# Places of expert 0 by counting ranks in the router loop, the remaining searches and the first down matrix moved behind the first gather

## The chip, the cores and the metric

The kernel runs on one core of one Trainium2 chip, as one launch. The metric is the device time in microseconds (us), smaller is better. The work is done by TensorE (PE in the profile: matrix products and transposes into PSUM, with the weight loads PEld beside them), VectorE (DVE), ScalarE (ACT), GpSimd (POOL) and the queues that start transfers (SP's, and POOL's own). Every engine runs its instructions strictly in the order that the program fixes when it is built.

## The reference, cut to what matters

One transformer block over 1024 tokens of width 1024: a mixer (gated linear attention beside a long convolution), a residual, and then a mixture of experts in which each expert picks its tokens. The change touches only the choice of tokens and what stands around it:

```python
aff  = softmax(h @ w_router)                      # 1024 tokens x 16 experts
vals, idx = top_k(aff.T, 128)                     # every expert takes its 128 best tokens
xs   = h[idx]                                     # gather, per expert 128 x 1024
hid  = silu(xs @ w_gate) * (xs @ w_up)            # per expert, 1024 x 1024 matrices
y    = (hid @ w_down) * vals
out  = zeros_like(h).at[idx].add(y)               # scatter-add, then residual and norm
```

The order of an expert's 128 tokens among themselves is free, as long as the same order is used for the gather, the values and the scatter.

## The kernel before, in words

Everything is float32. A product of two matrices is made of three products of rounded halves: `split` makes `hi` on ACT (L144) and `lo` on DVE (L147), `mm3` issues the three products on PE (L150 to L152). A weight matrix of an expert is loaded in 8 tiles of 128 x 1024 (`eraw` for gate and up, `erawl` for down), split into `ehi` and `elo`, and multiplied into a PSUM tile `pex`: 8 tiles, two halves, three products, so 48 `pex` products for a matrix and 144 for an expert's three. On PE the matrices come in the order gate(0), up(0), gate(1), down(0), up(1), gate(2), down(1) and so on. An expert's input needs a transposed copy of its gathered rows (`ptx` from `xs`, then `tt`, `thi`, `tlo`), and its down product a transposed copy of the hidden values (`ptx` from `sg`).

The router loop runs over the token tiles 7 down to 0: `gla_out`, `residual` and `router` are staggered, and `router(i)` ends with `aff[:, :, i]`, the 16 affinities of 128 tokens. When all of `aff` is there, `select(e0, ne, tag, bits)` finds for `ne` experts at once the 128th largest affinity bit by bit: each iteration compares `aff` with `2^bits - 1` thresholds (`gea` or `geb` on DVE), counts over the tokens with 8 products with a matrix of ones (`psel` on PE), and takes the largest threshold that still holds 128 tokens (`thr`, `base` on DVE). `select(0, 2, "a", 5)` takes 6 iterations, `select(2, 14, "b", 2)` takes 15. Then the mask (`gt`, `eq`, `need`, `keep`) and two rounds of prefix sums on PE give `pos`, the place of each token in its expert's list. `route(e)` turns `pos` into indices (`oh` on DVE, 8 small products `pi` on PE, `pv`, `ix`) and starts an indirect gather on POOL's queue. `tv` holds token numbers and the affinities in three bf16 parts for `pi`.

Two allocations matter here. The PSUM tag "t" has two buffers, which `pi` and `ptx` take in program order (and `psel` of search a before the change). The tag "ex" has three buffers of a full matrix, which `pex` takes, and `psel` of search b. `elo` has four buffers (`NLO`). The order within each engine is set by a list scheduler at build time, which follows data, buffers and estimated times; nothing is reordered when the kernel runs.

Of the kernel before, what the change touches and what calls it, by code (L numbers as in the profile page):

```python
# [10 lines left out]
F32 = mybir.dt.float32  # L11
# [9 lines left out]
P = 128  # L21
# [21 lines left out]
def shape_constants():  # L43
    f = np.float32
    out = {}
    quarter = D // 4
    omega = (1.0 / (f(10000.0) ** (np.arange(quarter, dtype=f) / f(quarter)))).astype(f)
    er = (np.arange(16, dtype=f)[:, None] * omega).astype(f)
    ec = (np.arange(64, dtype=f)[:, None] * omega).astype(f)
    out["posr"] = np.concatenate([np.sin(er), np.cos(er)], -1).astype(f)  # L50
    pc = np.concatenate([np.sin(ec), np.cos(ec)], -1).astype(f)
    out["posc"] = np.concatenate([pc, pc], 0)
    out["pos"] = np.concatenate([np.repeat(out["posr"], 64, 0), np.tile(out["posc"], (8, 1))], 1).reshape(8, 128, 1024)
    out["ident"] = np.eye(P, dtype=f)

    n1 = np.arange(8)[None, :, None]
    n2 = np.arange(128)[:, None, None]
    k2 = np.arange(128)[None, None, :]
    th = 2 * np.pi * (k2 + 0.5) * (n1 + 8 * n2) / 2048.0
    fc, fs = np.cos(th), -np.sin(th)  # L60
    out["fmat"] = np.stack([fc, fs], 1).astype(f)
    out["fneg"] = (-fs).astype(f)
    out["imat"] = np.stack([fc.transpose(2, 1, 0) / 1024.0, fs.transpose(2, 1, 0) / 1024.0], 1).astype(f)

    t = np.linspace(0.0, 1.0, L, dtype=f)[:, None]
    w = (f(2.0 * math.pi) * np.arange(L, dtype=f)[:, None] / f(L)).astype(f)
    bands = np.linspace(1e-4, 15, 16, dtype=f)[None, :]
    fw = (bands * w).astype(f)
    z = np.concatenate([t, np.cos(fw), -np.sin(fw)], -1).astype(f)
    n = (np.arange(8)[:, None] + 8 * np.arange(128)[None, :]).reshape(-1)  # L70
    out["zfeat"] = z[n].T.astype(f)
    deltas = np.abs(np.linspace(math.log(1e-2) / 1.5, math.log(1e-2) / 0.3, HYW, dtype=f))
    dec = np.exp(-t * deltas).astype(f)[n].reshape(8, 128, 4, 128)
    out["decay"] = dec.transpose(2, 1, 0, 3).astype(f)

    i16 = 1.0 / 16.0
    tok, col = np.meshgrid(np.arange(P), np.arange(2 * (CH + 2)), indexing="ij")
    pre = (tok // CH == col // (CH + 2)) & (tok % CH < col % (CH + 2))
    out["pre"] = (pre * i16).astype(f)
    ss, cc = np.meshgrid(np.arange(P) % CH, np.arange(CH), indexing="ij")  # L80
    out["smask"] = np.stack([ss <= cc, ss >= cc], 1).astype(np.int32)
    ss, cc = np.meshgrid(np.arange(P), np.arange(P), indexing="ij")
    out["before"] = (ss < cc).astype(f)
    out["slot"] = np.broadcast_to(np.arange(1, P + 1, dtype=f), (P, P)).copy()
    out["sel"] = np.tile(np.eye(32, E, dtype=f), (4, 1))
    tid = np.zeros((P, NT, 2), f)
    tid[:, :, 0] = np.arange(P)[:, None]
    tid[:, :, 1] = P * np.arange(NT)[None, :]
    out["tokid"] = tid
    for b in (5, 2):  # L90
        dig = np.zeros((P, 30 // b, 1 << b), np.int32)
        for i in range(30 // b):
            dig[:, i, :] = np.arange(1 << b) << (30 - b * (i + 1))
        out[f"digit{b}"] = dig
    return {"c_" + k: np.ascontiguousarray(v) for k, v in out.items()}
# [3 lines left out]
def tile_gla_hyena_moe(ctx: ExitStack, tc: tile.TileContext, io: dict, out: bass.AP):  # L99
# [826 lines left out]
    def wout_tile(k, tile_of, queue=SY):  # L926
        raw = mid_tile("woraw")
        queue.dma_start(raw, io["w_out"][0, k * P:(k + 1) * P, :])
        V.tensor_mul(raw, raw, m2)
        hi, lo = tile_of("wohi", F32R), tile_of("wolo", F32R)  # L930
        split(hi, lo, raw)
        return hi, lo
# [12 lines left out]
    def gb(tag, bufs):  # L945
        return lambda shape, name: psg.tile(shape, F32, name=name, tag=tag, bufs=bufs)

    ga, gc, gd, ge1 = gb("ga", 2), gb("gc", 2), gb("gd", 1), gb("ge", 1)

    def chunk_updates(i, e4, vs):  # L950
# [123 lines left out]
    befr = s2([P, P], name="befr")  # L1074
    SY.dma_start(befr, io["c_before"])
    V.tensor_copy(before, befr)
    ws = [wout_tile(k, op_tile) for k in range(4)]
    p2a.close()
    g2 = p2.enter_context(tc.tile_pool(name="g2", bufs=1, side="right", reuse_waits="tile"))

    def h4(shape, name, tag, bufs, dt=F32):
        return g2.tile(shape, dt, name=name, tag=tag, bufs=bufs)


    diag = [g2.tile([P, NH, P], F32, name=f"diag{x}") for x in range(2)]
# [98 lines left out]
        V.reciprocal(sm, sm)  # L1184
        V.tensor_scalar(aff[:, :, i], ex, sm, None, op0=ALU.mult)

    outs, rows = [], []
    for i in reversed(range(-2 - 1, NT)):
        if i >= 0:
            outs.append((i, gla_out(i)))  # L1190
        if rows:
            router(*rows.pop(0))
        if outs and (i < 0 or len(outs) > 1):
            o_ = outs.pop(0)
            rows.append((o_[0], *residual(*o_)))
    p2.close()
    st_stack.close()
    early_stack.close()
# [25 lines left out]
        queue.dma_start(raw, io[w][0, e, k * P:(k + 1) * P, :])  # L1224
        return raw

    loaded = {(w, k): expert_tile(w, 0, k) for w in ("w_gate", "w_up", "w_down") for k in range(KT)}

    def expert_mm(w, e, xt, between=None, at=KB):
        ps = pse.tile([P, D], F32, name="pex", tag="ex", bufs=3)  # L1230
# [14 lines left out]
    def select(e0, ne, tag, bits):  # L1245

        aff_ = aff[:, e0:e0 + ne]

        def tl(shape, dt, name, bufs=1):
            return mt(shape, dt, name + tag, name + tag, bufs)  # L1250

        def column_sums(ps, mask):
            for t in range(NT):
                T.matmul(ps, ones, mask[:, :, t], start=t == 0, stop=t == NT - 1)

        def prefix(ps, mask):
            T.matmul(ps, before, mask, start=True, stop=False)
            for s in range(1, NT):
                T.matmul(ps[:, :, s:], ones, mask[:, :, 0:NT - s], start=False, stop=s == NT - 1)

        if e0 == 0:
            def pr(n):
                return pT([P, n], "psel")
        else:
            acc = pse.tile([P, D], F32, name="psel", tag="ex", bufs=3)
            flip = [0]

            def pr(n):
                flip[0] ^= 512
                return acc[:, flip[0]:flip[0] + n]  # L1270

        base = tl([P, ne], F32, "base")
        V.memset(base, 0.0)
        nd = 1 << bits
        for b in range(30 // bits):
            thr = tl([P, nd, ne], F32, "thr", 2)
            V.tensor_tensor(thr.bitcast(I32), digit[bits][:, b, :, None].to_broadcast([P, nd, ne]),
                            base.bitcast(I32)[:, None, :].to_broadcast([P, nd, ne]), op=ALU.bitwise_or)
            ge = tl([P, nd - 1, ne, NT], BF16, "ge")
            V.tensor_tensor(ge, aff_[:, None].to_broadcast([P, nd - 1, ne, NT]),  # L1280
                            thr[:, 1:nd, :, None].to_broadcast([P, nd - 1, ne, NT]), op=ALU.is_ge)
            pc = pr((nd - 1) * ne)
            column_sums(pc, ge.rearrange("p q e t -> p (q e) t"))
            upper = thr[:, 1:nd].rearrange("p q e -> p (q e)")
            V.scalar_tensor_tensor(upper, pc, float(CAP) - 0.5, upper, op0=ALU.is_ge, op1=ALU.mult)
            V.tensor_reduce(base, thr.rearrange("p q e -> p e q"), AX.X, ALU.max)
        thb = base[:, :, None].to_broadcast([P, ne, NT])
        gt = tl([P, ne, NT], BF16, "gt")
        V.tensor_tensor(gt, aff_, thb, op=ALU.is_gt)
        eq = tl([P, ne, NT], BF16, "eq")  # L1290
        V.tensor_tensor(eq, aff_, thb, op=ALU.is_equal)
        pg_ = pr(ne)
        column_sums(pg_, gt)
        need = tl([P, ne], F32, "need")
        V.tensor_scalar(need, pg_, -1.0, float(CAP), op0=ALU.mult, op1=ALU.add)
        pq_ = pr(ne * NT).rearrange("p (e t) -> p e t", t=NT)
        prefix(pq_, eq)
        keep = tl([P, ne, NT], BF16, "keep")
        V.tensor_tensor(keep, pq_, need[:, :, None].to_broadcast([P, ne, NT]), op=ALU.is_lt)
        V.tensor_mul(keep, keep, eq)  # L1300
        V.tensor_add(keep, keep, gt)
        pp = pr(ne * NT).rearrange("p (e t) -> p e t", t=NT)
        prefix(pp, keep)
        V.scalar_tensor_tensor(pos[:, e0:e0 + ne], pp, 1.0, keep, op0=ALU.add, op1=ALU.mult)

    NF = 2
    select(0, NF, "a", 5)

    tv = mp.tile([P, E, NT, 5], BF16, name="tv")
    V.tensor_copy(tv[:, :, :, 0:2], tokid[:, None].to_broadcast([P, E, NT, 2]))  # L1310
# [8 lines left out]
    def route(e):  # L1319
        pi = pT([P, 5], "pi")  # L1320
        oh = mt([P, NT, P], BF16, "oh", "s2", NS)
        V.tensor_tensor(oh, slot[:, None, :].to_broadcast([P, NT, P]),
                        pos[:, e, :, None].to_broadcast([P, NT, P]), op=ALU.is_equal)
        for t in range(NT):
            T.matmul(pi, oh[:, t], tv[:, e, t], start=t == 0, stop=t == NT - 1)
        ix = tiny.tile([P, 1], I32, name="ix", bufs=4)
# [31 lines left out]

    A.preload_act_table_set("silu_and_others")
    routed = [route(0)]  # L1360
    xt = transposed(0, routed[0][2], True)
    routed.append(route(1))
    select(NF, E - NF, "b", 2)
    with tc.issue_after(routed[0][3].ins):
        sg = gate_part(0, xt)
    m5 = row_of(5, mp)
# [81 lines left out]
```

## Time and profile before

| what | value |
|---|---|
| time, median of 3 runs | 1380.2 us (1378.26 to 1383.59) |
| time of the profiled execution | 1380.59 us |
| its span, first to last instruction | 1378.8 us |
| mean granted TensorE clock | 0.964 |
| PE busy | 1276.7 us (93%) |
| DVE busy | 1149.8 us (83%) |
| ACT busy | 805.8 us (58%) |
| router loop and its tail | until 736 us |
| searches, first gather | 736 to 768 us |
| expert products | 768 to about 1353 us |

The profiled execution is one of the ordinary ones: its time is 0.4 us above the median, and 1.8 us of it lie outside the span. Times inside the span are given in us from its start. A row of the timeline gives start, duration, engine, line, operation, output and inputs, and in brackets how long the engine was idle before it and what released it. [...]

### The profile page before, as it was taken

How to read it: one execution, taken by the hardware profiler on the slowest of the kernel's cores; microseconds unless marked ns; L12 is line 12 of the kernel's file. 1: busy time of each engine (PE TensorE's matmuls, PEld its weight loads, DVE VectorE, ACT ScalarE, POOL GpSimd, SP SyncE). 2: the span in 40 equal slices, each digit the busy share in tenths (PEclk: the TensorE clock that was granted, in tenths of full speed). 3: DMA queues.
4: the chain of work that ended last, by engine and by line, in shares of the span. 5: the costliest groups of instructions: out<-in, count | busy, mean ns of one | idle time of the engine just before them, and what ended most of it. 6: DMA issues, size and time to landing. Idle time of an engine off the chain costs nothing.

```text
span 1378.8 us, 21543 instructions
## 1 busy us (share of the span) xinstructions
PE 1276.7 (93%) x7720; PEld 1044.5 (76%) x7720; DVE 1149.8 (83%) x1920; ACT 805.8 (58%) x1228; POOL 129.9 (9%) x142
## 2 busy tenths in 40 slices
PE   6988999999999998988996899999999999999982
PEld 4777888688898897766775678888888888877762
DVE  6877938899778678788656799999999999988886
ACT  3247453121211314886553678888888888877864
POOL 1020000010100110001000000001111111012010
PEclk9998999999999998999996899999999999999996
DMA  7993551774746545676768789999999999999765
GB/s 213 325 230 123 167 145 42 234 199 150 202 152 185 141 113 176 159 165 186 242 230 337 244 318 357 361 394 383 387 385 386 390 385 391 369 365 370 264 202 225
DMA packets 154362, 354.81 MB, mean 257 GB/s; under 512 B 28389, under 2 KB 74013, under 8 KB 153999
## 3 DMA queue, kind: packets, MB, share of 16 engines
q1 hardware_dynamic: 134911, 292.84, 59.7%
q0 software_dynamic: 19344, 60.61, 15.8%
q8 instruction: 60, 0.98, 0.3%
q14 instruction: 47, 0.39, 0.1%
HBM read 310.89 MB, written 50.89 MB: 262 GB/s over the span
## 4 chain that ended last, share of the span: by engine, by line
PE 70%; issue 9%; DMA 7%; DVE 7%; ACT 5%; POOL 1%; SPq 1%; POOLq 0%; DVEq 0%; ACTq 0%
PE pex L151 13%; PE pex L152 12%; PE pex L150 12%; PE phy L543 3%; PE phy L542 3%; PE phy L545 3%; PE ptx L1343 2%; PE pdft L467 2%; PE pdft L468 2%; PE pvg L150 2%; PE pm L334 2%; PE pvg L152 1%; PE pvg L151 1%; PE pdft L671 1%; DMA wt<-w_ada 1%
## 5 line engine op out<-in xcount | busy, mean ns | idle before, releaser
L147 DVE TENSOR_TENSOR elo<-eraw,ehi 128x1024 fp32r<-128x1024 f32 x256 | 302.5, 1221 | 13.2 <-issue 6.0
L151 PE MATMUL pex<-elo,thi 128*128 128x512 f32 x768 | 306.4, 399 | 4.8 <-DVE elo L147 4.4
L150 PE MATMUL pex<-ehi,thi 128*128 128x512 f32 x768 | 305.8, 398 | 2.3 <-ACT thi L144 1.3
L152 PE MATMUL pex<-ehi,tlo 128*128 128x512 f32 x768 | 303.4, 395 | 0.8 <-DVE tlo L147 0.8
L144 ACT ACTIVATE ehi<-eraw 128x1024 fp32r<-128x1024 f32 x256 | 265.0, 1068 | 50.2 <-PE pex L152 49.3
L151 PEld LDWEIGHTS pex<-elo,thi 128*128 128x128 f32 x768 | 145.3, 189 | 40.3 <-DVE elo L147 10.5
L150 PEld LDWEIGHTS pex<-ehi,thi 128*128 128x128 f32 x768 | 145.3, 189 | 33.9 <-ACT thi L144 1.7
L152 PEld LDWEIGHTS pex<-ehi,tlo 128*128 128x128 f32 x768 | 145.3, 189 | 31.6 <-DVE tlo L147 1.2
L147 DVE TENSOR_TENSOR elo<-erawl,ehi 128x1024 fp32r<-128x1024 f32 x128 | 149.5, 1221 | 6.2 <-ACT ehi L144 5.3
L144 ACT ACTIVATE ehi<-erawl 128x1024 fp32r<-128x1024 f32 x128 | 131.3, 1057 | 19.6 <-PE pex L152 17.4
L144 ACT ACTIVATE whi<-wraw 128x1024 fp32r<-128x1024 f32 x30 | 31.8, 1059 | 104.6 <-DMA wraw<-w_in 29.6
L542 PE MATMUL phy<-xh,whi 128*128 128x512 f32 x192 | 77.2, 402 | 12.2 <-ACT whi L144 12.2
L543 PE MATMUL phy<-xl,whi 128*128 128x512 f32 x192 | 76.1, 396 | 0.0
L150 PE MATMUL pvg<-whi,xh 128*128 128x256 f32 x256 | 73.3, 286 | 0.0
L151 PE MATMUL pvg<-wlo,xh 128*128 128x256 f32 x256 | 72.5, 283 | 0.0
L152 PE MATMUL pvg<-whi,xl 128*128 128x256 f32 x256 | 72.5, 283 | 0.0
L1389 POOL DMA_INDIRECT d_acc<-y,ix x15 | 34.6, 2308 | 392.4 <-DVE y L1388 392.4
L1348 ACT ACTIVATE tt<-ptx,fcol,gfcol 128x128 f32<-128x128 f32 x128 | 48.7, 463 | 34.1 <-PE ptx L1343 34.1
L545 PE MATMUL phy<-xh,wlo 128*128 128x512 f32 x192 | 61.9, 400 | 0.0
L438 ACT ACTIVATE D<-pdft 128x512 f32<-128x512 f32 x32 | 19.1, 597 | 70.9 <-PE pdft L468 40.7
L147 DVE TENSOR_TENSOR wlo<-wraw,whi 128x1024 fp32r<-128x1024 f32 x30 | 36.7, 1222 | 22.5 <-ACT whi L144 22.5
L467 PE MATMUL pdft<-kk,fmat 128*128 128x128 f32 x256 | 52.7, 289 | 0.3 <-ACT D L438 0.2
(452 smaller groups left out, 2601.1 us busy)
## 6 DMA issues: line engine op xcount, KB each, us to landing
eraw<-w_gate SPq DMA_DIRECT2D x128, 512.0 KB
eraw<-w_up SPq DMA_DIRECT2D x128, 512.0 KB
erawl<-w_down SPq DMA_DIRECT2D x128, 512.0 KB
wt<-w_ada SPq DMA_DIRECT2D x48, 512.0 KB
wraw<-w_in SPq DMA_DIRECT2D x30, 512.0 KB
kspec<-d_spec SPq DMA_DIRECT2D x16, 512.0 KB
xt<-x SPq DMA_DIRECT2D x8, 512.0 KB
d_spec<-ue POOLq DMA_DIRECT2D x8, 512.0 KB, 6.0
```

What stands on the lines that cost most here:

```text
L144: A.activation(hi, src, AF.Copy)
L147: V.tensor_sub(lo, src, hi.bitcast(F32))
L150: T.matmul(out_, lh, rh, start=first, stop=False)
L151: T.matmul(out_, lh, rl, start=False, stop=False)
L152: T.matmul(out_, ll, rh, start=False, stop=last)
L334: T.matmul(pm[32 * g:32 * g + 32, 256 * h:256 * h + 256], sc[:, k], wt[:, 256 * g:256 * g + 256], start=k == ks[0] and h == 0, stop=k == k ...
L467: T.matmul(ps[:, r], fmat[:, r, m1], kk[m1 // 4][:, 0, m1 % 4], start=True, stop=False)
L542: T.matmul(ps[:, h], hi[:, k], rh[k][:, h], start=k == 0, stop=False)
L543: T.matmul(ps[:, h], hi[:, k], rl[k][:, h], start=False, stop=False)
L545: T.matmul(ps[:, h], lo[:, k], rh[k][:, h], start=False, stop=k == KT - 1)
L1348: A.activation(tt[:, k], pt[:, k], AF.Identity, bias=fcol[:, 0, kk_:kk_ + 1], scale=gfcol[:, kk_:kk_ + 1])
L1389: G.indirect_dma_start(out=d_acc[:, :], out_offset=bass.IndirectOffsetOnAxis(ap=ix[:, :1], axis=0), in_=y, in_offset=None, compute_op=ALU.add)
```

## The change

Four things are edited.

- `rank(i)` and `rank_sums(i, over)` are new, for the first `NF = 1` expert. In the router loop, a tile behind `router`, the affinities of expert 0 in tile i are laid along a row (`prow`, a transpose on PE; `arow`), and every token of tile i is compared with all tokens of tiles i to 7 (`over` on DVE, 128 to 1024 columns, with the count in `cnt`; `tie` breaks equal values inside the tile by the constant `after`). `rank_sums`, a tile later, subtracts from the ranks of the later tiles what the products `pbelow` of `over` with a column of ones say. Over the loop these are 8 transposes and 28 small products. At the end `pos0` is the place of every token for expert 0, without a search.
- `route(0)` takes `pos0`. The `select` for the first two experts is gone from the place before `tv`. Expert 1 alone is searched by `select(1, 1, "a", 5)`, which stands behind `transposed(0)` in the program; `route(1)` and `select(2, 14, "b", 2)` follow as before.
- All searches now keep `psel` in a tile of the tag "ex".
- The 8 tiles of w_down of expert 0 are loaded by POOL's queue behind the first gather, and no longer by SP's queue ahead of it.

```diff
+    arow = g2.tile([P, NF, L], F32, name="arow")
...
+    def rank(i):
+        W = (NT - i) * P
+        for e in range(NF):
+            row = gc([P, P], name="prow")
+            T.transpose(row, aff[:, e, i:i + 1].to_broadcast([P, P]), ident)
+            V.tensor_copy(arow[:, e, i * P:(i + 1) * P], row)
+            a_ = aff[:, e, i:i + 1]
+            over = h4([P, L], "over", "over", 2, BF16)
+            cnt = tiny.tile([P, 2], F32, name="cnt")
+            V.tensor_scalar(over[:, 0:W], arow[:, e, i * P:], a_, 0.0, op0=ALU.is_gt, op1=ALU.add, accum_out=cnt[:, 0:1])
+            tie = s2([P, P], BF16, name="tie")
+            V.scalar_tensor_tensor(tie, arow[:, e, i * P:(i + 1) * P], a_, after, op0=ALU.is_equal, op1=ALU.mult,
+                                   accum_out=cnt[:, 1:2])
+            V.scalar_tensor_tensor(rk[:, e, i:i + 1], cnt[:, 0:1], cnt[:, 1:2], rk[:, e, i:i + 1], op0=ALU.add, op1=ALU.add)
+            overs.append((i, over))
+
+    def rank_sums(i, over):
+        if i + 1 < NT:
+            below = gc([P, NT], name="pbelow")
+            for t in range(i + 1, NT):
+                T.matmul(below[:, t:t + 1], over[:, (t - i) * P:(t - i + 1) * P], ones[:, 0:1], start=True, stop=True)
+            V.tensor_sub(rk[:, 0, i + 1:], rk[:, 0, i + 1:], below[:, i + 1:])
+        if i == 0:
+            V.scalar_tensor_tensor(pos0[:, 0], rk[:, 0], CAP + 0.5, rk[:, 0], op0=ALU.is_le, op1=ALU.mult)
...
         if rows:
+            ranks.append(rows[0][0])
             router(*rows.pop(0))
         if outs and (i < 0 or len(outs) > 1):
             o_ = outs.pop(0)
             rows.append((o_[0], *residual(*o_)))
+        while len(ranks) > 1 or ranks == [0]:
+            rank(ranks.pop(0))
+            if len(overs) > 1:
+                rank_sums(*overs.pop(0))
+    rank_sums(*overs.pop(0))
...
-    loaded = {(w, k): expert_tile(w, 0, k) for w in ("w_gate", "w_up", "w_down") for k in range(KT)}
+    loaded = {(w, k): expert_tile(w, 0, k) for w in ("w_gate", "w_up") for k in range(KT)}
...
-        if e0 == 0:
-            def pr(n):
-                return pT([P, n], "psel")
-        else:
-            acc = pse.tile([P, D], F32, name="psel", tag="ex", bufs=3)
...
+        acc = pse.tile([P, D], F32, name="psel", tag="ex", bufs=3)
...
-    NF = 2
-    select(0, NF, "a", 5)
...
-                        pos[:, e, :, None].to_broadcast([P, NT, P]), op=ALU.is_equal)
+                        (pos0[:, e] if e < NF else pos[:, e])[:, :, None].to_broadcast([P, NT, P]), op=ALU.is_equal)
...
     routed = [route(0)]
+    with tc.issue_after(routed[0][4].ins):
+        loaded.update({("w_down", k): expert_tile("w_down", 0, k, G) for k in range(KT)})
     xt = transposed(0, routed[0][2], True)
+    select(1, 1, "a", 5)
     routed.append(route(1))
-    select(NF, E - NF, "b", 2)
+    select(2, E - 2, "b", 2)
```

The scheduler moves more than the diff shows. On VectorE, at the end of search b, around the splits of expert 1's gate matrix and expert 0's down matrix, this stood before (`gtb`, `eqb`, `needb`, `keepb`, `pos`: the mask and places of experts 2 to 15):

```order
L1289 TENSOR_TENSOR gtb<-aff,baseb 128x112
L1291 TENSOR_TENSOR eqb<-aff,baseb 128x112
L1377 TENSOR_TENSOR sg<-pex,sg 128x1024
L1295 TENSOR_SCALAR needb<-psel 128x14
L147 TENSOR_TENSOR elo<-eraw,ehi 128x1024
L1299 TENSOR_TENSOR keepb<-psel,needb 128x112
L147 TENSOR_TENSOR elo<-eraw,ehi 128x1024
L1300 TENSOR_TENSOR keepb<-keepb,eqb 128x112
L147 TENSOR_TENSOR elo<-eraw,ehi 128x1024
L1301 TENSOR_TENSOR keepb<-keepb,gtb 128x112
L147 TENSOR_TENSOR elo<-eraw,ehi 128x1024
L1304 SCALAR_TENSOR_TENSOR pos<-psel,keepb 128x112
```

The same steps stand there now, from the last splits of the down matrix (`erawl`) on; the pattern of four rows from `geb` to `thrb` stands five times in all ahead of `gtb`, of which the first and last are shown:

```order
L148 TENSOR_TENSOR elo<-erawl,ehi 128x1024
L1316 TENSOR_TENSOR thrb<-digit_6047,baseb 128x56
L148 TENSOR_TENSOR elo<-erawl,ehi 128x1024
L1319 TENSOR_TENSOR geb<-aff,thrb 128x336
L1324 SCALAR_TENSOR_TENSOR thrb<-psel,thrb 128x42
L1325 TENSOR_REDUCE baseb<-thrb 128x14
...
L1319 TENSOR_TENSOR geb<-aff,thrb 128x336
L1324 SCALAR_TENSOR_TENSOR thrb<-psel,thrb 128x42
L1325 TENSOR_REDUCE baseb<-thrb 128x14
L1328 TENSOR_TENSOR gtb<-aff,baseb 128x112
L1330 TENSOR_TENSOR eqb<-aff,baseb 128x112
L1334 TENSOR_SCALAR needb<-psel 128x14
```

Before, the steps of the search lie between splits; now the last five iterations and the mask stand in a row behind the fourth split of the down matrix, with nothing else between them.

On TensorE, where the transposes of the hidden values of expert 0 (`ptx` from `sg`) stand, before, with the last of the products that place expert 2 (`pi`) ahead of them; the `pex` around them are the last of gate(1):

```order
L1325 LDWEIGHTS oh
L1325 MATMUL pi<-tv,oh 128x5
L151 MATMUL pex<-elo,thi 128x512
L152 MATMUL pex<-ehi,tlo 128x512
L1343 MATMUL ptx<-ident,sg 128x128 x4
L150 MATMUL pex<-ehi,thi 128x512
L1343 MATMUL ptx<-ident,sg 128x128 x4
L151 MATMUL pex<-elo,thi 128x512
L152 MATMUL pex<-ehi,tlo 128x512
```

and now, where the `pex` behind them are the first of down(0):

```order
L1302 LDWEIGHTS ones
L1302 MATMUL psel<-keepb,ones 128x14
L1362 LDWEIGHTS oh
L1362 MATMUL pi<-tv,oh 128x5
...
L1380 MATMUL ptx<-ident,sg 128x128 x8
L151 MATMUL pex<-ehi,thi 128x512
L152 MATMUL pex<-elo,thi 128x512
L153 MATMUL pex<-ehi,tlo 128x512
```

Before, 132 `pex` stand ahead of the first of these transposes and 12 more before down(0) begins. Now all 144 stand ahead, and between the 144th and the transposes stand, with no `pex` among them, five groups of `psel` for `geb`, those for `gtb`, `eqb` and `keepb`, and the 8 `pi` of expert 2. Ahead of the first `pex` there are now 3 groups for `gea` and 2 for `geb` (before 6 and 9); between the first and the 144th there are 3 groups for `gea` (at the 7th, 19th and 32nd `pex`), 8 for `geb`, and the small ones for `gta`, `eqa`, `keepa` (before 6 for `geb` and the small ones for `gtb`, `eqb`, `keepb`). `pi` of expert 1 stands at the 60th `pex` (before the 2nd), `ptx` of expert 1 at the 81st (before the 66th).

On POOL's queue the first gathers stood in a row before:

```order
L1159 DMA d_h<-hh 128x1024
L1151 DMA d_acc<-xres 128x1024
L1159 DMA d_h<-hh 128x1024
L1333 DMA xs<-d_h,ix 128x1024 x3
L1389 DMA d_acc<-y,ix 1024x1024
```

and now:

```order
L1169 DMA d_h<-hh 128x1024
L1161 DMA d_acc<-xres 128x1024
L1169 DMA d_h<-hh 128x1024
L1370 DMA xs<-d_h,ix 128x1024
L1267 DMA erawl<-w_down 128x1024 x8
L1370 DMA xs<-d_h,ix 128x1024 x2
L1429 DMA d_acc<-y,ix 1024x1024
```

Eight loads have come between the first and the second gather.

## Rows read from the trace of the kernel before

**Rows 1.** Busy us and count of each engine, granted clock, DMA share, GB/s, by stretch.

```profile
660.00:700.00 40.00, 39.07 (x298) 29.43 (x297) 24.92 (x97) 25.15 (x87) 4.31 (x8) 1.00 0.63 217
736.00:760.00 24.00, 12.93 (x144) 11.40 (x143) 19.91 (x77) 4.43 (x5) 1.08 (x2) 0.50 0.68 273
768.00:800.00 32.00, 31.69 (x184) 24.67 (x185) 27.07 (x53) 24.98 (x33) 1.44 (x1) 0.94 0.68 232
```

**Rows 2.** Chain that ended last, router to first products: start us, us, what.

```profile
735.91 0.28 DVE aff L1185
757.50 0.38 PE pi L1325 x8
759.13 5.14 DMA xs<-d_h,ix
764.41 1.10 PE ptx L1343 x4
767.96 0.80 PE pex L150
769.19 0.22 PE pi L1325 x8
770.47 0.43 PE pex L151
```

**Rows 3.** VectorE's timeline at the end of search a (search b beside it).

```profile
752.78 0.22 DVE L1285 SCALAR_TENSOR_TENSOR thra<-psel,thra 128x62 f32<-128x62 f32 x1 [0.48 <-PE psel L1254]
754.21 0.51 DVE L1280 TENSOR_TENSOR geb<-aff,thrb 128x336 bf16<-128x336 f32 x1
755.58 0.20 DVE L1285 SCALAR_TENSOR_TENSOR thrb<-psel,thrb 128x42 f32<-128x42 f32 x1 [0.37 <-PE psel L1254]
756.10 0.22 DVE L1277 TENSOR_TENSOR thrb<-digit,baseb 128x56 int32<-128x56 int32 x1
756.23 1.22 DVE L1322 TENSOR_TENSOR oh<-slot,pos 128x1024 bf16<-128x1024 bf16 x1
757.92 0.17 DVE L1328 COPY pv<-pi 128x5 f32<-128x5 f32 x1
```

**Rows 4.** VectorE, two lines in SBUF: duration ns min/median/max, first to last start.

```profile
L233 DVE TENSOR_SCALAR sn<-sy x4: 415/420/429, 9.9 to 18.5; 64x512 f32<-64x512 f32 x2, 128x512 f32<-128x512 f32 x2
L1314 DVE CAST tv<-rest x2: 349/350/350, 737.5 to 738.6; 128x128 bf16<-128x128 f32 x2
```

**Rows 5.** TensorE's timeline in the products of expert 0.

```profile
782.46 0.39 PE L150 MATMUL pex<-ehi,thi 128*128 128x512 f32 x1
782.69 0.40 PE L151 MATMUL pex<-elo,thi 128*128 128x512 f32 x1
782.93 0.78 PE L1254 MATMUL psel<-geb,ones 128*128 128x42 bf16 x8
783.49 0.48 PE L152 MATMUL pex<-ehi,tlo 128*128 128x512 f32 x1
810.97 0.40 PE L150 MATMUL pex<-ehi,thi 128*128 128x512 f32 x1
```

**Rows 6.** POOL's timeline: last store of d_h, gathers (xs), scatters (d_acc).

```profile
735.68 0.53 POOL L1159 DMA_DIRECT2D d_h<-hh  x1 [3.61 <-ACT ex L1183]
770.58 1.44 POOL L1333 DMA_INDIRECT xs<-d_h,ix  x1 [10.19 <-DVE geb L1280]
895.90 2.31 POOL L1389 DMA_INDIRECT d_acc<-y,ix  x1 [26.36 <-DVE y L1388]
1212.42 2.31 POOL L1389 DMA_INDIRECT d_acc<-y,ix  x1 [26.94 <-DVE y L1388]
1259.63 5.86 POOL L1333 DMA_INDIRECT xs<-d_h,ix  x1 [5.17 <-issue]
1327.68 2.29 POOL L1389 DMA_INDIRECT d_acc<-y,ix  x1 [34.87 <-DVE y L1388]
```

**Rows 7.** The 16 gathers, last line of the tile's view.

```profile
DMA to landing us min/median/max: 4.7/7.9/12.9
```

More of the change, by code (lines that the diff above doesn't have):

```diff
@@ L83, in shape_constants @@
     out["before"] = (ss < cc).astype(f)
+    out["after"] = (ss > cc).astype(f)
     out["slot"] = np.broadcast_to(np.arange(1, P + 1, dtype=f), (P, P)).copy()
@@ L946, in gb @@
         return lambda shape, name: psg.tile(shape, F32, name=name, tag=tag, bufs=bufs)
+    NF = 1
     ga, gc, gd, ge1 = gb("ga", 2), gb("gc", 2), gb("gd", 1), gb("ge", 1)
@@ L1076, in tile_gla_hyena_moe @@
     V.tensor_copy(before, befr)
+    after = keep.tile([P, P], F32, name="after")
+    SY.dma_start(after, io["c_after"])
+    pos0 = keep.tile([P, NF, NT], BF16, name="pos0")
+    rk = keep.tile([P, NF, NT], F32, name="rk")
+    V.tensor_scalar(rk, tokid[:, None, :, 1].to_broadcast([P, NF, NT]), 1.0, None, op0=ALU.add)
     ws = [wout_tile(k, op_tile) for k in range(4)]
@@ L1185, in router @@
         V.tensor_scalar(aff[:, :, i], ex, sm, None, op0=ALU.mult)
-    outs, rows = [], []
+    def rank(i):
[21 more added lines that the diff above has]
+            V.scalar_tensor_tensor(pos0[:, 0], rk[:, 0], CAP + 0.5, rk[:, 0], op0=ALU.is_le, op1=ALU.mult)
+    outs, rows, ranks, overs = [], [], [], []
     for i in reversed(range(-2 - 1, NT)):
@@ L1259, in prefix, with pr @@
                 T.matmul(ps[:, :, s:], ones, mask[:, :, 0:NT - s], start=False, stop=s == NT - 1)
-        if e0 == 0:
-            def pr(n):
-                return pT([P, n], "psel")
-        else:
-            acc = pse.tile([P, D], F32, name="psel", tag="ex", bufs=3)
[L1266 to L1270, printed above, removed]
+        acc = pse.tile([P, D], F32, name="psel", tag="ex", bufs=3)
+        flip = [0]
+        def pr(n):
+            flip[0] ^= 512
+            return acc[:, flip[0]:flip[0] + n]
         base = tl([P, ne], F32, "base")
```

## The prediction, made blind

> **What bounds the kernel now.** I read the windows first. In the router loop TensorE is busy for 39.07 of 40 us at full clock, and from 768 on, where the expert products have begun, for 31.69 of 32 [rows 1]. Both stages are bound by PE: what is put on PE there lengthens the kernel, and what another engine does there is free while it keeps up. Between them lies a stretch that PE does not bind. From 736 to 760 it is busy for 12.93 of 24 us, at a granted clock of 0.50, with VectorE at 19.91. The chain of waits tells what sets its length: `aff` of the last tile at 735.91, the two searches, `pi` of expert 0 at 757.50, the gather at 759.13, its landing after 5.14, `ptx` at 764.41, the first `pex` at 767.96 [rows 2]. So 23.2 us pass from `aff` to the gather and 8.8 from there to the first product. The change shortens the first part.
>
> The second thing to read is what search b costs where nothing covers it, and it stands in VectorE's timeline at the end of search a: `geb` at 754.21, the step that takes up PE's counts at 755.58, the next thresholds at 756.10 [rows 3]. With their own 0.22 and a handover to the next `geb`, an iteration takes 2.14 us from end to end, of which PE works 0.78. In the stage of products these steps lie between splits, and PE pays only for the insertion of the 8 `psel`: from 782.69 to 783.49 pass 0.80 where two `pex` are 0.23 apart (782.46 to 782.69), so 0.57 a group [rows 5].
>
> **The front: 11.9 us gained at the first product.**
> *Router loop, +1.3.* Six of the 8 `prow` and 15 of the 28 `pbelow` fall into the loop, where PE has no room. Four transposes took 1.10 at half clock [rows 2], so 0.14 each at full clock; a pair of weight load and narrow product took 0.03 in `pi` (0.22 for 8 [rows 2]) and 0.07 in `psel` (0.57 for 8). 0.84 plus 0.45 to 1.05; I take the narrow pair, since `pbelow` has one column.
> *Router tail, +1.6.* The order on VectorE puts the ranks of tiles 2 and 1 ahead of the norm of tile 0, on which its affinities wait: two `over` passes of 768 and 896 columns and two `tie`. No row shows this operation. A one-input step in SBUF took 0.42 for 512 columns, `oh` with two inputs 1.22 for 1024 [rows 3, 4]. A pass of 1024 lies between 0.69 (0.42, and 512 more columns at twice the rate of `oh`, about 0.27) and 1.22. With the ties this makes 1.7 to 2.7, and about 1 us of it falls into time in which VectorE waits for ACT there: 1.4 to 1.9 late, I take 1.6.
> [...]
> *From `aff` of tile 0 to `pos0`, 3.2.* `aff` 0.28, `prow` 0.27, its copy about 0.35, `over` 0.69 to 1.22, seven `pbelow` at half clock 0.4, and three or four short steps at 0.2 with their handovers: 2.9 to 3.5.
> *From `pos0` to the gather, 5.2.* The casts and remainders of `tv`, which used to run beside the search, now stand behind `pos0`, and `pi` waits for the last: six at 0.35 (0.27 apart, as they overlap), `oh` 1.22, and five short steps between them, 3.5 to 3.9; `pi` 0.38; from `pv` at 757.92 to the gather at 759.13 1.2 [rows 2 to 4].
> So `aff` to gather takes 8.4 in place of 23.2, a gain of 14.8, less 1.3 and 1.6: 11.9. The gather would start at 747.2, land after 5.1 and let the first `pex` start near 756.0. A landing as slow as the median of all 16 gathers, 7.9, would take back 2.8 [rows 7].
> *Loads of w_down, 0.* A transfer issued on POOL took 0.53 [rows 6], 8 of them 4.2, so POOL is done near 753 and the second gather, near 780, doesn't feel them. 4 MB at the 273 GB/s of [rows 1] take 15 us, so they land by 768 to 770; the first split of down(0) is due some 36 us after the first product, near 792. That is the cover. SP's queue is the shorter by them.
>
> **From the first product to the first down product: 23.8 us lost.** Before, down(0) began at 810.97, 43.0 after the first `pex` [rows 2, 5]. Now:
> *More groups, +2.5.* Two more `geb` groups and three of `gea` between the 144 products, 0.57 each, less one `pi` group of 0.22.
> *Second gather, +2.5.* `pi` of expert 1 moves from the 2nd to the 60th product, about 21 us in; with `oh`, a split ahead of `pv`, and the 1.2 to the gather, that starts 23.7 in. Landing takes 5.1 to 7.9; PE reaches `ptx` of expert 1, at the 81st, 27 in. It waits 1.8 to 4.6, and for nothing if all of this is 2 us sooner. Queued behind `ptx` is all of gate(1).
> *A third holder of the tag "ex", +0.5.* With two `psel` tiles and gate's `pex` all three buffers are taken, so up(0) waits for the silu that frees one (0 to 1.5).
> So PE has done its 144th product 48.5 in.
> *The stop, 18.3.* The transposes of `sg` share the tag "t" with `pi`, and `pi` of expert 2 stands ahead of them. That needs all of search b, five iterations of which the order puts behind the 144th product on PE, and on VectorE behind the fourth split of down(0), whose `elo` buffer that product frees. So in a row: split and `geb` 1.65, `psel` 0.78, four iterations at 2.14 (8.6), then from the last counts to `pi` what search a took, 752.78 to 757.50 [rows 2, 3], 4.7, and 0.5 for masks of 14 experts in place of 2, `pi` 0.38, and from `ptx` to the first `pex` 1.7 (764.41 to 767.96 is 3.55 [rows 2], of which the `tt` step, 1.85, is absent here). PE has nothing else: all further `pex` are queued behind.
> 48.5 + 18.3 - 43.0 = 23.8.
> *Clock, +1.7.* [...] The 0.94 of 768:800 makes 3.8 us at half clock [rows 1], which cost 1.8 over full. The stop would repeat it.
> *The last experts, -2.* From 895.90 to 1212.42 nine scatters came every 35.2 us, and the last three every 38.4 to 1327.68 [rows 6]: late in the kernel the scheduled order places gathers and transposes ahead of where they are ready. In the new order this begins one expert later. One expert less is worth 3.2; it may as well fall elsewhere (-5 to +2).
>
> **Sum.** -11.9 + 23.8 + 1.7 - 2 = +11.6, on the profiled execution's 1380.6: 1392.2. That execution lies 0.4 over the median, so 1392 is given. The ends: a front gain of 9 to 13, a stall of 0 to 4.6, a stop of 16 to 21, and -5 to +2 make 1386 to 1398.
>
> **Rivals.**
> *The stop is given back (faster).* While PE stands still, loads and splits run ahead. If the products after it were held by those, they would go faster than before and repay the 20 us of stop and clock: 1392 - 20 = 1372. For it: at 810.97 and around, splits are close behind PE. Against: PE has 31.69 of 32 us [rows 1], and four `elo` buffers hold 12 products' worth, 3 us. It decides at the scatters: they must come less than 35.2 apart for several experts. 0.08.
> *About even.* The order of the last experts loses all its irregularity: 3 x 3.2 = 9.7 regained in place of 2: 1384. For it: the change shifts the pattern already; against: some of it is still seen in the new order. 0.18.
> *POOL delays the second gather.* The gather at 1259.63 held POOL for 5.86, the one at 770.58 for 1.44 [rows 6]. Were each of the 8 loads held so, POOL would be busy for 47 us, until 795; the second gather would start 15 later, PE would wait for it at the 81st product, and the time would be 1407. It decides if POOL isn't free by 780. [...] 0.07.
> *The ranks save nothing.* The passes of the tail cost so much that the gather starts as late as before: 1392 + 12 = 1404. It would take 15 us of ranks behind the loop, where I count under 6. 0.05.
>
> **Numbers.** The forecast has 0.62. Measurement tells 0.5%, 6.9 us, from no change: slower is above 1387. Slower takes most of the forecast and the last two rivals, 0.78 with a small part of the even case; faster 0.08; same 0.14. The range goes from below the even case, 1380, to 1400, which leaves out the faster rival and the two slow ones.
>
> **What would show it.** The first `pex` near 756 and the gather near 747 show the front. A gap on PE of 2 to 5 us ahead of `ptx` of expert 1, and one of 16 to 20 us ahead of `ptx` from `sg`, near 805 to 822, at a granted clock of 0.50, with only `geb`, `thrb` and `baseb` on VectorE, show the loss. Scatters from the third on should lie about 13 to 14 us later than before. I am wrong if that stop is short, since the other terms nearly cancel.

## The result and the profile after

The changed kernel takes 1392.43 us (median of 4 runs, 1389.79 to 1394.27), the kernel before 1379.23 (4 runs): a ratio of 1.0085, 95% interval 1.0065 to 1.0105. It is slower by 13 us. The profiled execution has a span of 1391.4 (1378.8 before).

The same stretches as in [rows 1], and as a fourth the one in which the loss lies (busy us and count of PE, PEld, DVE, ACT and POOL, granted clock as a share of full speed, DMA share, GB/s):

```profile
660.00:700.00 40.00, 39.05 (x299) 29.33 (x298) 27.35 (x108) 25.16 (x87) 4.32 (x8) 1.00 0.62 211
736.00:760.00 24.00, 9.79 (x80) 7.87 (x81) 17.45 (x63) 10.65 (x20) 6.19 (x10) 0.56 0.77 287
768.00:800.00 32.00, 29.57 (x196) 23.15 (x195) 27.38 (x55) 22.61 (x29) 1.48 (x1) 1.00 0.77 268
803.80:824.70 20.90, 8.61 (x85) 7.04 (x83) 12.58 (x36) 1.66 (x2) 0.66 (x1) 0.58 0.36 136
```

The router loop is as full as before and the first product comes in the second stretch now, but TensorE, which had 31.69 of 32 us between 768 and 800, has 29.57, and from 803.8 to 824.7 it works for 8.61 of 20.9 us at a clock of 0.58.

The chain of waits, with the steps of [rows 2] and the second gather (start us, us, what):

```profile
739.12 0.30 DVE aff L1195
745.68 0.27 PE pi L1362 x8
747.40 5.73 DMA xs<-d_h,ix
753.18 1.13 PE ptx L1380 x4
756.76 0.80 PE pex L151
781.26 5.84 DMA xs<-d_h,ix
787.15 1.10 PE ptx L1380 x8
```

The last store of the residual ahead of the router loop comes at 642.52 and 642.61 in the two executions, so times up to here compare directly. From `aff` to the gather now take 8.3 us (23.2 before); the first product starts at 756.76 in place of 767.96. That is the gain, 11.2 us.

The stop on TensorE's timeline, from the 144th product to the first of down(0), in the order that the program lists:

```profile
804.30 0.39 PE L153 MATMUL pex<-ehi,tlo 128*128 128x512 f32 x1
807.89 0.78 PE L1297 MATMUL psel<-geb,ones 128*128 128x42 bf16 x8 [3.20 <-DVE geb L1319]
810.03 0.78 PE L1297 MATMUL psel<-geb,ones 128*128 128x42 bf16 x8 [1.36 <-DVE geb L1319]
...
816.47 0.78 PE L1297 MATMUL psel<-geb,ones 128*128 128x42 bf16 x8 [1.36 <-DVE geb L1319]
818.13 0.38 PE L1297 MATMUL psel<-gtb,ones 128*128 128x14 bf16 x8 [0.88 <-DVE gtb L1328]
...
822.52 0.38 PE L1362 MATMUL pi<-tv,oh 128*128 128x5 bf16 x8 [1.63 <-DVE oh L1359]
822.76 1.95 PE L1380 MATMUL ptx<-ident,sg 128*128 128x128 f32 x8
824.54 0.79 PE L151 MATMUL pex<-ehi,thi 128*128 128x512 f32 x1
825.13 0.63 PE L152 MATMUL pex<-elo,thi 128*128 128x512 f32 x1
```

Each later `psel` waits 1.36 us for VectorE's next `geb`, at a step of 2.145 us: iterations with nothing beside them. VectorE's timeline, from the 144th product to the second bare iteration, shows what the first one waits 3.20 us for:

```profile
804.94 1.21 DVE L148 TENSOR_TENSOR elo<-erawl,ehi 128x1024 fp32r<-128x1024 f32 x1
806.20 1.22 DVE L148 TENSOR_TENSOR elo<-erawl,ehi 128x1024 fp32r<-128x1024 f32 x1
807.34 0.50 DVE L1319 TENSOR_TENSOR geb<-aff,thrb 128x336 bf16<-128x336 f32 x1
...
809.47 0.51 DVE L1319 TENSOR_TENSOR geb<-aff,thrb 128x336 bf16<-128x336 f32 x1
```

Down(0) starts 67.8 us after the first product, 43.0 before [rows 2, 5].

POOL's timeline, to set beside [rows 6]:

```profile
747.40 1.35 POOL L1370 DMA_INDIRECT xs<-d_h,ix  x1 [7.97 <-PE psel L1297]
748.75 3.78 POOL L1267 DMA_DIRECT2D erawl<-w_down  x7
...
781.26 1.48 POOL L1370 DMA_INDIRECT xs<-d_h,ix  x1 [27.31 <-PE pex L152]
...
910.79 2.30 POOL L1429 DMA_INDIRECT d_acc<-y,ix  x1 [26.36 <-DVE y L1428]
...
1227.83 2.30 POOL L1429 DMA_INDIRECT d_acc<-y,ix  x1 [25.28 <-DVE y L1428]
...
1263.44 2.30 POOL L1429 DMA_INDIRECT d_acc<-y,ix  x1 [26.05 <-DVE y L1428]
...
1301.93 2.30 POOL L1429 DMA_INDIRECT d_acc<-y,ix  x1 [31.54 <-DVE y L1428]
1339.44 2.28 POOL L1429 DMA_INDIRECT d_acc<-y,ix  x1 [35.22 <-DVE y L1428]
```

The seven loads in a row took 3.78 us, 0.54 each. The scatter that came at 895.90 comes at 910.79, 14.9 late; the one at 1212.42 at 1227.83; the last at 1339.44 in place of 1327.68, 11.8 late. So the order of the last experts gives 3 us back: two scatters now come 38.5 and 37.5 us after the one ahead of them, where before three did so, by 39.7, 38.3 and 37.2; the irregular end begins one expert later, as forecast.

### The profile page after: what moved, and what is told of

Its sections match the earlier page's. It is cut to its first block, busy times and chain, and to the rows that moved or that the text cites. A ratio compares the mean times of both kernels' runs of the same rounds, so it can differ in the third digit from the quotient of the medians.

```text
span 1391.4 us, 21690 instructions
## 1 busy us (share of the span) xinstructions
PE 1279.5 (92%) x7756; PEld 1045.1 (75%) x7756; DVE 1160.0 (83%) x1977; ACT 808.0 (58%) x1228; POOL 131.2 (9%) x150
## 4 chain that ended last, share of the span: by engine, by line
PE 46%; DVE 4%; ACT 1%; issue 1%; DMA 1%; POOLq 0%; DVEq 0%; ACTq 0%
PE pex L152 13%; PE pex L151 12%; PE pex L153 12%; PE ptx L1380 2%; PE pout L152 1%; PE pout L153 1%; PE pout L151 1%; DMA xs<-d_h,ix 1%; PE psel L1297 1%; DVE elo L148 1%; DVE xf L1456 1%; ACT tt L1385 1%; PE po L1135 0%; PE pth L1178 0%; DVE state L636 0%
## 5 line engine op out<-in xcount | busy, mean ns | idle before, releaser
L152 PEld LDWEIGHTS pex<-elo,thi 128*128 128x128 f32 x768 | 145.2, 189 | 37.2 <-DVE elo L148 6.8
L439 ACT ACTIVATE D<-pdft 128x512 f32<-128x512 f32 x32 | 19.1, 596 | 69.6 <-PE pdft L469 39.7
L1385 ACT ACTIVATE tt<-ptx,fcol,gfcol 128x128 f32<-128x128 f32 x128 | 48.4, 465 | 19.1 <-PE ptx L1380 19.1
```

Source lines behind the costliest of these rows:

```text
L152: T.matmul(out_, lh, rl, start=False, stop=False)
L1385: A.activation(tt[:, k], pt[:, k], AF.Identity, bias=fcol[:, 0, kk_:kk_ + 1], scale=gfcol[:, kk_:kk_ + 1])
```

## The experiments

All ratios are to the kernel before, run on the same chip. Where stages of different kernels are compared, times are counted from the first product or from the last store of the residual ahead of the router loop, since the loop begins up to 3 us earlier or later from one profiled execution to another (that store starts at 639.3 to 644.6); why is not known. This table has the start of the nth `pex` in us after the start of the first, counted on TensorE's timeline:

| `pex` number | before | changed | order (1) | a for two (2) | 3 bits (5) | a for two, late transposes (7) |
|---|---|---|---|---|---|---|
| 49, up(0) | 14.5 | 18.9 | 18.8 | 21.1 | 18.6 | 21.1 |
| 82, behind `ptx` of expert 1 | 25.1 | 31.3 | 31.3 | 37.6 | 30.2 | 30.9 |
| 145, down(0) | 43.0 | 67.8 | 48.8 | 58.1 | 67.4 | 52.0 |
| 193, up(1) | 54.7 | 80.5 | 61.3 | 71.0 | 80.3 | 65.0 |
| 241, gate(2) | 66.8 | 92.9 | 92.4 | 84.3 | 92.6 | 78.2 |

**1. Is it the order in the shared tag, or the late search?** `pi` of expert 2 is put behind the transposes of `sg`:

```diff
-            if e + 2 < E:
+            if 0 < e < E - 2:
                 routed.append(route(e + 2))
...
+            def sg_rows():
+                ahead.append(transposed(e, sg))
+                if e == 0:
+                    routed.append(route(2))
```

> The changed kernel, but expert 2 is routed behind the transposes of expert 0's hidden values, so these no longer stand behind pi of expert 2 in the PSUM tag. Theory A (search b is simply late, whoever waits for it): no stop at the 144th product, where the transposes now stand at the 109th and 132nd; instead gate(2), at the 240th product, waits for the last iteration, mask, pi, gather and transposes of expert 2, 17 to 20 us, and the time stays at 1388 to 1393. Theory B (only the order in the shared tag costs the stop): the stop is gone, no wait over 5 us in its place, 1370 to 1375.

1392.55 us, ratio 1.0091 (1.0074 to 1.0108). Down(0) starts at 48.8, so the stop at the 144th product is gone; but up(1) to gate(2) take 31.1 us in place of 12.2. TensorE's timeline at the 240th product:

```profile
833.24 0.38 PE L1297 MATMUL psel<-gtb,ones 128*128 128x14 bf16 x8 [2.89 <-DVE gtb L1328]
...
838.40 0.37 PE L1362 MATMUL pi<-tv,oh 128*128 128x5 bf16 x8 [1.63 <-DVE oh L1359]
844.51 1.97 PE L1380 MATMUL ptx<-ident,xs 128*128 128x128 f32 x8 [5.74 <-DMA xs<-d_h,ix]
848.08 0.79 PE L151 MATMUL pex<-ehi,thi 128*128 128x512 f32 x1 [1.60 <-ACT thi L145]
```

The end of the last iteration, and mask, `pi`, gather and transposes of expert 2 stand there, and TensorE works for 5.1 of the 18.9 us to 848.1. Theory A holds: the shared tag only says which product pays for the late search.

**2. Expert 2 taken out of search b.**

```diff
-    select(1, 1, "a", 5)
+    select(1, 2, "a", 5)
     routed.append(route(1))
-    select(2, E - 2, "b", 2)
+    select(3, E - 3, "b", 2)
```

> The changed kernel, but search a takes experts 1 and 2, and search b experts 3 to 15, which then isn't needed before expert 3, one expert (35 us) later. Theory A (the stop is expert 2's wait for search b): no idle time of TensorE over 4 us from the first product to the 288th; wider gea groups add 1 us; 1370 to 1375. Theory B (TensorE stops because five iterations have no other work to lie beside, and they will stand bare wherever the search ends): the stop comes back one expert later and the time is 1386 to 1392.

1385.12 us, ratio 1.0034 (1.002 to 1.0048), between the two. No stop of that kind is left, so the cause by A is right, but 10 to 15 us of the expected gain are not there. The two longest waits of TensorE up to gate(2), on its timeline:

```profile
790.37 1.30 PE L1380 MATMUL ptx<-ident,xs 128*128 128x128 f32 x8 [4.05 <-DMA xs<-d_h,ix]
801.57 1.10 PE L1380 MATMUL ptx<-ident,sg 128*128 128x128 f32 x8 [0.74 <-DVE sg L1417]
```

The scheduler now puts `ptx` of expert 1 at the 70th product, and the gather lands 4 us later than that. Behind this wait the granted clock is at 0.50 once more, from 791.1 to 794.5 (products 0.43 us apart there, 0.23 behind it), which costs about 1.7 us, half of that stretch. The rest is in the table: 49 products take 21.1 us in place of 14.5, with no wait of TensorE over 0.3 us. Among them lie 7 groups of searches a and b (3 for `gea` with 62 columns, 4 for `geb`) and the small ones of search a, where before there were 2; and the granted clock is at 0.50 for 9.4 us from the first product, for 4.0 before (last section).

**3. What the ranks cost.** `rank` and `rank_sums` in the kernel before, result unused:

```diff
     for i in reversed(range(-2 - 1, NT)):
...
+        while len(ranks) > 1 or ranks == [0]:
+            rank(ranks.pop(0))
+            if len(overs) > 1:
+                rank_sums(*overs.pop(0))
+    rank_sums(*overs.pop(0))
```

> The kernel before, with the ranks of expert 0 counted in the router loop as in the changed kernel but not used: search a still takes experts 0 and 1. Theory A (ranks cost 1.3 us in the loop and 1.6 to 1.9 behind it, all on the path): 1382 to 1383.5 where the kernel before has 1379.5 to 1380. Theory B (they fall into idle time): within 0.7 us of the kernel before. Affinities of tile 0 at 738.8 to 739.2 by A, at 736 by B.

1388.1 us, ratio 1.0056 (1.0039 to 1.0073): 5 to 10 us, more than by either theory. On VectorE's timeline, between `aff` and the first thresholds, stand the ranks of the last tile:

```profile
739.87 0.28 DVE L1194 TENSOR_SCALAR aff<-ex,sm 128x16 f32<-128x16 f32 x1
741.05 1.28 DVE L1207 TENSOR_SCALAR_CACHE_REDUCE over<-arow,aff 128x1024 bf16<-128x1024 f32 x1
743.11 0.17 DVE L1221 SCALAR_TENSOR_TENSOR pos<-rk 128x8 bf16<-128x8 f32 x1
743.41 0.21 DVE L1319 TENSOR_TENSOR thra<-digit,basea 128x64 int32<-128x64 int32 x1
```

From `aff` to `thra` pass 3.5 us, 0.4 before. I had left this third part out of the expectation. From the last store of the residual ahead of the loop to `aff` the execution takes 1.9 us more than before, to the gather 5.7, to the first product 6.1, which is within the interval.

**4. The loads of w_down back on SP's queue.**

```diff
-    loaded = {(w, k): ... for w in ("w_gate", "w_up") for k in range(KT)}
+    loaded = {(w, k): ... for w in ("w_gate", "w_up", "w_down") for k in range(KT)}
...
-    with tc.issue_after(routed[0][4].ins):
-        loaded.update({("w_down", k): expert_tile("w_down", 0, k, G) for k in range(KT)})
```

> The changed kernel, but with w_down of expert 0 loaded by SP's queue ahead of the first gather, as before the change. Theory A (these loads are hidden on either queue): within 1.5 us of the changed kernel, 1391 to 1394. Theory B (4 MB ahead of the gather delay the stores of h or the gather's landing, so that the move itself earns something): the first product 2 to 5 us later, 1394 to 1397.

1392.92 us, ratio 1.0098 (1.0081 to 1.0115), as the changed kernel. From gather to `ptx` pass 7.8 us in place of 5.8, with the DMA engines at 1.03 of their time against 0.74, so the move did earn 2 us at the first product. By up(1) only 0.6 of it is left: the stop ends with the search, not with the products.

**5. Fewer iterations.** Search b with 3 bits a step (and a table of digits for 3):

```diff
-    select(2, E - 2, "b", 2)
+    select(2, E - 2, "b", 3)
```

> The changed kernel, but search b takes 3 bits at a time: 10 iterations with 7 thresholds in place of 15 with 3. One iteration is left behind the 144th product, where five were. Theory A (the stop is made of bare iterations of 2.14 us and a fixed rest of about 11): the stop falls from 20.0 to 12 to 13 us (four iterations less, the one left about 1 us longer), the groups among the products, wider, cost 1 us more: 1384 to 1387. Theory B (the stop ends with something else than the last iteration): above 1390.

1393.88 us, ratio 1.0098 (1.0081 to 1.0115), a time that B had given. TensorE's timeline around one of the groups among the products, and then at the stop:

```profile
784.77 0.39 PE L152 MATMUL pex<-elo,thi 128*128 128x512 f32 x1
785.00 1.56 PE L1297 MATMUL psel<-geb,ones 128*128 128x98 bf16 x8
786.26 0.54 PE L153 MATMUL pex<-ehi,tlo 128*128 128x512 f32 x1
...
808.55 0.39 PE L153 MATMUL pex<-ehi,tlo 128*128 128x512 f32 x1
811.28 1.56 PE L1297 MATMUL psel<-geb,ones 128*128 128x98 bf16 x8 [2.35 <-DVE geb L1319]
813.88 0.38 PE L1297 MATMUL psel<-gtb,ones 128*128 128x14 bf16 x8 [1.03 <-DVE gtb L1328]
...
818.27 0.38 PE L1362 MATMUL pi<-tv,oh 128*128 128x5 bf16 x8 [1.63 <-DVE oh L1359]
820.29 0.79 PE L151 MATMUL pex<-ehi,thi 128*128 128x512 f32 x1
```

The stop is 11.5 us (808.8 to 820.3), from 20.0, a little under what A gave. But the 144th product comes 8.1 us later than in the changed kernel: a group with 98 columns pushes the products apart by 1.26 (786.26 - 784.77 - 0.23) where one of 42 costs 0.57. Seven such groups stand among the products, eight of 42 columns in the changed kernel, which makes 4.3 of it. Of the rest, TensorE waits 3.8 us in this stretch in place of 2.4, and its granted clock is at 0.50 for 9.6 us in place of 6.2, since it falls twice more (last section), for about 1.7. What was taken from the stop was paid ahead of it.

**6. Both: search a for two experts and 3 bits.**

```diff
-    select(1, 1, "a", 5)
+    select(1, 2, "a", 5)
...
-    select(2, E - 2, "b", 2)
+    select(3, E - 3, "b", 3)
```

> Search a for experts 1 and 2 and search b for experts 3 to 15 with 3 bits at a time. Theory A (what is left of the loss, once the stop is gone, is the price of groups that the products enclose, 0.57 us each, and the wait for the second gather): 8 groups of b in place of 13 at some 0.75 each save 1 to 1.5 us over the run with 2 bits (1385.1), and the transposes of expert 1, at the 78th product in place of the 70th, wait 1 to 2 us less: 1381 to 1384. Theory B (groups are hidden beside the splits that bound the stage): as with 2 bits, 1384 to 1387.

1388.78 us, ratio 1.0054 (1.0037 to 1.0071), slower than with 2 bits. Groups are not hidden, so far A holds; its price was wrong, since it goes by columns (1.26 us for 98 in run 5, 0.57 for 42) more than by count, and wider groups lose.

**7. Search a for two experts, transposes of expert 1 later.** To edit 2 comes

```diff
-        pu = expert_mm("w_up", e, xt, next_rows, KU)
+        pu = expert_mm("w_up", e, xt, next_rows, KU if e else 6)
```

> Search a for experts 1 and 2, and the transposes of expert 1's gathered rows written later in the program, so that they stand at the 90th product and not at the 70th. Theory A (TensorE waits at the 70th for the second gather, which costs 4 to 5 us, and at the 90th it has landed): 1380 to 1382 where the run with the transposes at the 70th had 1385.1. Theory B (the wait goes over to the first products of gate(1) for want of thi, or to the splits): 1384 to 1386.

1377.67 us (10 runs), ratio 0.9986 (0.9976 to 0.9997): by the ratios 14 us under the changed kernel and, by a little, the only version under the kernel before, and better than A gave. The 82nd product comes at 30.9 in place of 37.6: the wait of 4.05 is gone, the clock, which fell behind it in run 2, stays at 1.00 (worth 1.7 us; products 0.23 us apart there), and the transposes themselves now stand behind this product (0.9). In place of the wait for the gather there is one for `thi` at the first product of gate(1):

```profile
789.57 0.50 PE L151 MATMUL pex<-ehi,thi 128*128 128x512 f32 x1 [0.63 <-ACT thi L145]
```

**8. All three edits** (5, 2 and 7 together).

> All three edits: search a for experts 1 and 2, search b in steps of 3 bits, transposes of expert 1 at the 90th product. Theory A: both savings add, 1378 to 1381, so level with the kernel before or a little under it. Theory B (one of the two is not there): 1381 to 1385.

1388.59 us, ratio 1.0059 (1.0043 to 1.0076). With 3 bits the late transposes bring gate(2) from 85.3 us after the first product (run 6) to 83.1, and the times of the two runs are level all the same; where the 2 us go is not shown. Wide groups and waits have cost 23.4 us up to the 49th product (21.1 in run 7).

**9. The late transposes alone,** the last edit in the kernel before.

> The kernel before with one edit: the transposes of expert 1's gathered rows written later, so that they stand at the 90th product and not at the 66th. Theory A (the late place earns something only where the gather is late; before the change it landed long ahead): within 0.2% of the kernel before, 1378 to 1383. Theory B (the place earns something by itself): 1374 to 1377, and the version with search a for two experts and late transposes owes its lead to it.

1382.18 us (12 runs), ratio 1.0007 (0.9993 to 1.002): no gain. The late place paid only where the gather was late, by 4.05 us in run 2.

**10. The search for expert 1 in its old place,** ahead of `tv`:

```diff
+    select(1, 1, "a", 5)
     tv = mp.tile([P, E, NT, 5], BF16, name="tv")
...
-    select(1, 1, "a", 5)
     routed.append(route(1))
```

> The changed kernel, but the search for expert 1 stands in its old place ahead of tv; only the ranks take expert 0 out of it. Theory A (the front gain comes from the ranks, since pi of expert 0 no longer depends on a search, and not from moving the search): first product 1 to 2 us later than in the changed kernel, 10 us earlier than before the change; six iterations stand bare in place of five, so the time is 1394 to 1398. Theory B (the search has to be moved to earn the front): first product within 3 us of the kernel before, and 1400 or more.

1392.26 us, ratio 1.0085 (1.0063 to 1.0107). The gather starts 0.6 us later in the loop's time than in the changed kernel and the first product 0.5 earlier. So the front gain is the ranks' alone. The stop is 0.8 longer (21.1 from the start of the 144th product to that of the 145th, 20.2 in the changed kernel), not 2.1, since VectorE reached the first bare iteration earlier: the time is under what A gave.

## Why the prediction was right

1392 was forecast and 1392.43 came, by the forecast's own mechanism. That it fits to half a microsecond is luck: the terms are off by up to 1.1, and these errors cancelled.

| term | forecast | measured |
|---|---|---|
| first product | -11.9 | -11.2 |
| first product to 145th | +23.8 | +24.8 |
| clock after the stop | +1.7 | +1.5 |
| last experts | -2 | -3.1 |

The measured terms add up to 12.0; the span grew by 12.6, and the rest lies mostly behind the last scatter. The 1.7 for the clock was an estimate from the 3.8 us at half clock of [rows 1]. Behind the stop of the changed kernel products start 0.43 us apart from 825.13 to 827.69 and 0.23 from 827.96 on; the 3.2 us at the slower pace, from 824.54, make the 1.5.

*The front.* Loop and tail were sized a little high. The last d_h store came 3.2 late (735.68 to 738.90), forecast 2.9, but 0.9 of that lies ahead of the loop's first store of `d_acc` (662.01 before, 662.92 now), where no rank stands yet; the stretch ahead of that store takes 19.1 us in run 8, 19.5 in the kernel before and 20.3 in the changed one. From that store on the ranks cost 2.3, in the changed kernel as in run 3: 1.0 in the loop (forecast 1.3) and 1.3 in the tail (1.6, whose bounds were added up wrongly: 1.7 to 2.7 less 1 is 0.7 to 1.7, not 1.4 to 1.9). From `aff` to the gather 8.3 were measured, 8.4 forecast, but of different parts. VectorE's timeline, the ranks of the last tile:

```profile
740.30 1.28 DVE L1208 TENSOR_SCALAR_CACHE_REDUCE over<-arow,aff 128x1024 bf16<-128x1024 f32 x1
741.51 0.35 DVE L1210 SCALAR_TENSOR_TENSOR tie<-arow,aff,after 128x128 bf16<-128x128 f32 x1
742.36 0.17 DVE L1222 SCALAR_TENSOR_TENSOR pos<-rk 128x8 bf16<-128x8 f32 x1
```

`over` took 1.28 for 1024 columns, above my high end of 1.22. In this form, with a count and a bf16 result, it went at the pace of `oh` (1.22 for 1024 [rows 3]) and not at that of `sn` (0.42 for 512 [rows 4]), on which I had built the low end of 0.69: 1.01, 1.15 and 1.28 us for 768, 896 and 1024 columns are 1.05 ns a column. Behind the gather 0.5 were lost: 5.8 us to `ptx` in place of 5.3. Without the 0.9 ahead of the loop's first store the first product would have come 12.1 earlier.

*To the 144th product,* 48.5 forecast, 47.8 measured. The second gather cost 1.59 us of TensorE's idle time (forecast 2.5), the wait ahead of up(0), for the silu and for a `geb`, 0.8 (0.5), and the slow clock, of which nothing was reckoned there, about 1 more than before (6.2 us at 0.50 in place of 4.0, with products 0.43 us apart there and 0.23 behind). Left out the other way: the transposes of `sg`, which used to push the products of this stretch apart by 0.8 in all, no longer stand in it.

*The stop,* 18.3 forecast, 20.0 measured. The part that was too small is the first: from the end of the 144th product to the first bare `psel` 3.4 us, not 1.65. I had put only the fourth split ahead of `geb`; VectorE still had the third and the fourth to do, and the steps between. The fourth, at 806.20, follows without idle time, so it did not wait for the `elo` buffer of the 144th product, as I had it: VectorE was behind with its own work. The four iterations took 8.58 (8.6), from the last `psel` to `pi` 6.05 (6.0), from `pi` to `pex` 2.0 (2.1).

*The rivals.* The stop was not given back: scatters after it came 35.2 to 35.5 us apart, as before. The bound that I set against it was off by half: a weight tile takes six products, so four `elo` buffers hold 24 products' worth, 5.6 us. POOL did not hold up the second gather: it was idle for 27 us ahead of it. The last experts stayed irregular, so the even case did not come, and the ranks did save the time in front.

*The cause,* by experiments 1 and 2: experts need `pos` from a search that now ends behind the first product; whichever product needs it first waits. Run 1 moved the stop, run 2 removed it. What is argued and not shown apart is how the 6.6 us that run 2 loses in its first 49 products divide between groups and clock.

## What to carry to other kernels

A stretch in which the bounding engine idles is not only a loss: nine groups of search b lay ahead of the first product before the change, with TensorE busy for 12.93 of 24 us [rows 1], and once moved under the bounded stage each cost its full insertion (0.57 us a group here, 1.26 for one of over twice the width) and lost the pace of a chain that runs end to end (a group every 2.145 us in the stop, every 4.6 to 7.1 among the products of the changed kernel). Before a search is moved behind the work that it feeds, find the first consumer of its result in each engine's order and count the iterations left at that point: in the changed kernel TensorE stopped there for 20.0 us, with the transposes of `sg` behind `pi` of expert 2 in its order; they came at 822.76, though `sg` was written by 793.0, and run 1 did them from 794.20 on. And once the front is shorter, re-place what was timed to the old one: a later place for one group of transposes was worth 7 us in run 7, the version that came out below both kernels, if only by 0.1% below the kernel before.

## What the hardware showed that I had not expected

The time that TensorE stays at half clock after its first expert product is not the same in kernels that begin the stage alike: 4.0 us before the change, 6.2 after it, 9.4 in run 2, and in run 5, whose groups are wider, 2.8. Windows of run 5 and then of run 2 (columns as above):

```profile
752.90:754.90 2.00, 2.00 (x8) 1.55 (x6) 1.25 (x4) 1.64 (x4) 0.00 (x0) 0.50 1.03 424
754.90:756.90 2.00, 2.00 (x9) 1.58 (x8) 2.00 (x6) 1.03 (x1) 0.00 (x0) 0.80 1.02 418
```

```profile
763.80:765.80 2.00, 2.00 (x6) 1.41 (x5) 2.00 (x3) 0.72 (x1) 0.00 (x0) 0.50 1.01 406
765.80:767.80 2.00, 2.00 (x19) 1.68 (x18) 0.26 (x2) 0.34 (x1) 0.00 (x0) 0.64 1.01 375
```

TensorE is busy for the whole of these windows, the clock still changes at 755.7 in the one, 2.8 us after the first product, and at 767.2 in the other, 9.4 after it. The clock also fell again among the products. In run 2 it is at 0.50 from 791.1 to 794.5, just behind the wait of 4.05 us for the gather; in run 5 from 772.7 to 776.2, behind a wait of 1.42 us for `gta`, and from 793.2 to 796.6, with products 0.42 to 0.44 us apart in these stretches; runs 6, 8 and 10 show such a pace once each ahead of down(0), near 784, 782 and 784. Behind the wait of 1.59 us for the second gather in the changed kernel it stays at 1.00, so the length of the wait alone does not decide it. What does, and what decides how long the first stretch lasts, the runs don't tell apart.
